# Loading the second product's weights on GpSimd's queue: one hybrid encoder, one core

## The chip, the cores and the metric

The kernel runs on one core of one Trainium2 chip. The metric is the device time of one execution in microseconds (us), from its first to its last instruction and what the launch lays around them.

## The reference

Four post-norm residual layers over x (512 tokens of 1024 features, float32): a bidirectional gated DeltaNet, an MLP, a bidirectional gated linear attention, an MLP.

```python
# DEPTH 2, layer i: token mixer i mod 2, then the MLP; alpha = 4 ** 0.25
x = layernorm(alpha * x + mixer_i(x))             # gated DeltaNet, then gated linear attention
x = layernorm(alpha * x + square(relu(x @ w1)) @ w2)   # w1: 1024 x 4096, w2: 4096 x 1024
```

The change touches the MLPs and the constants of the linear attention.

## The kernel before, in words

Every product is made in full float32 accuracy out of pieces: an operand is split into a high part (a cast on ACT, L90: `wh`, `w2h`, `ah`) and a low part (a subtraction on DVE, L91: `wl`, `w2l`, `al`), and TensorE does three products for one (L109 to L111).

The stages follow one another: DeltaNet up to about 455 us, the first MLP to about 790, linear attention to about 1057, the second MLP to the end. They overlap at the seams.

An MLP (`mlp`) handles its 4096 hidden features in four groups of eight column blocks ("features", f 0 to 7). For a feature, TensorE multiplies the input (`xth`, `xtl`) with a tile of w1 (`wst`, 512 KB, issued by SP at L45, three buffers) into a PSUM bank (`pj`, two of them), and ACT evicts it as relu and square into `h` (L276 and L277). The first four features of the first group are made in halves, since the input arrives in parts. The eighth feature waits for the bank of the sixth, and so on, so a late eviction on ACT holds TensorE.

The second product, of `h` with w2, is done for the groups 0 to 2 by Winograd's form of Strassen's scheme: seven products instead of eight. A group's rows of w2 are four blocks, (i, j) = (0,0), (0,1), (1,1) and (1,0), here A, B, C and D; each is two tiles `w2r` of 512 KB (q = 0 and 1: A0, A1 and so on; E0 and E1 are block (0,0) of the next group), out of a ring of ten. The block sums that the scheme needs are made in place by accumulating DMAs on GpSimd's queue (`plus`, L303, `w2r<-w2r`): first A += B and B += C, later A += C and D += A. Since each reads what a load has brought, it waits for that load, and the second pair waits for the first. Each `w2r` tile is also split into `w2h` and `w2l` (three buffers).

In the first group of an MLP, then, SP loads `wst` tiles and `w2r` tiles in one in-order queue, GpSimd (POOL) loads the layer norm's parameters (`ln`, L173) and issues the accumulations, and ACT has the splits' casts and the evictions in one order. The order on each engine is that of a scheduler, which takes instructions as the code issues them and as their operands come ready. `order` rows below show it; a name in front of an arrow is the tile written, the ones behind it are read.

In the first MLP, `extra` makes the constants of the linear attention at the same time (`GlaConst`): masks `mu` out of a temporary `tmp` that POOL fills (a memset and two affine selects), of which DVE takes the difference to the one before as 8-bit integers (L483 and L485), and two small loads, `gb` and `gcol`, on POOL's queue.

Of the kernel before, what the change touches and what calls it, by code (L numbers as in the profile page):

```python
# [12 lines left out]
AF = mybir.ActivationFunctionType  # L13
ALU = mybir.AluOpType
# [3 lines left out]
P = 128  # L18
# [232 lines left out]
def mlp(c, w1, w2, g, b, out=None, extra=None):  # L251
# [7 lines left out]
    tc, nc = c.tc, c.nc  # L259
    V, A, T = nc.vector, nc.scalar, nc.tensor  # L260
    G = 4
    GF = FF // G // P
    HF = GF // 2
    HT = S // 2
    with c.banks(pj=2, X=2, Y=2, Z=2), tc.tile_pool(name="mlp", bufs=2) as pool:
# [8 lines left out]

        def act(ps, h):
            A.activation(h, ps, AF.Relu)  # L276
            A.activation(h, h, AF.Square)  # L277

        def raw():
            return pool.tile([P, 2, 512], F32, name="w2r", tag="w2r", bufs=10)  # L280

        def load(gi, i, j):
            for q in range(2):
                blocks[i, j, q] = t = raw()
                r = (gi * GF + i * HF + 2 * q) * P
                c.dma(t, w2[r:r + 2 * P, 512 * j:512 * j + 512].rearrange("(k p) n -> p k n", p=P))

        def split(i):

            i_, j_ = {1: (0, 0), 2: (1, 0), 3: (1, 1), 4: (1, 0), 5: (0, 0), 6: (0, 0), 7: (0, 1)}[i]  # L290
            parts[i] = [c.split(blocks[i_, j_, q], [P, 2, 512], pool=ring("w2")) for q in range(2)]

            if i == 1:
                plus((0, 0), (0, 1))
                plus((0, 1), (1, 1))
            elif i == 5:
                plus((0, 0), (1, 1))
                plus((1, 0), (0, 0))
# [6 lines left out]
        def new_h():  # L305
            return [pool.tile([P, HF, S], F32, name="h", tag="h", bufs=3) for _ in range(2)]

        def feature(gi, f, h):
            act(c.proj_cm(w1, (gi * GF + f) * P, "pj"), h[f // HF][:, f % HF, :])

        def pair(src, where="ah"):
            return c.split(src, [P, HF, HT], pool=ring(where))
# [9 lines left out]
        def quarters(h):  # L322
            return [h[j][:, :, HT * i:HT * i + HT] for i in range(2) for j in range(2)]

        def second(gi, h, a, nxt):
# [19 lines left out]
            def fetch(i, j):  # L345
                if gi + 2 < G:
                    load(gi + 1, i, j)

            X, Y = banks("X"), banks("Y")
            load(gi, 1, 0)  # L350
            product(X, a, 1, True)
            for j in range(2):
# [71 lines left out]
        h = new_h()  # L424
        specs = [(c.wcols(w1, f * P, pool=ring("ah") if f == 3 else None), "pj", ("pj", "pj", "X", "X")[f]) for f in range(4)]
        for f, ps in enumerate(c.proj_halves(specs)):
            act(ps, h[0][:, f, :])
        for f in range(4, GF):
            feature(0, f, h)
            if f == 5:  # L430
                load(0, 0, 0)
                load(0, 0, 1)
            if f == 6:
                load(0, 1, 1)
                split(1)
                a = pair(quarters(h)[0])
        if extra:
            extra(lambda: pool.tile([P, P], F32, name="tmp", tag="tmp", bufs=2))
        for gi in range(G - 1):
            more = gi + 2 < G  # L440
            nh = new_h()
            todo = iter(range(GF))

            def nxt():
                f = next(todo)
                feature(gi + 1, f, nh)
                if f == 6 and more:
                    split(1)
                    nxt.a = pair(quarters(nh)[0])

            second(gi, h, a, nxt)
            h, a = nh, nxt.a if more else None
# [13 lines left out]
def sel_masks(c, pool, tmp):  # L466

    nc = c.nc
    out = {}
    prev = None  # L470
    for w in (1, 2, 4, 8, 16, 32, 64, 128):
        f = tmp().rearrange("p (a b) -> p a b", b=w)
        nc.gpsimd.memset(f, 1.0)
        if w < P:
            nc.gpsimd.affine_select(out=f, in_=f, compare_op=ALU.is_ge, fill=0.0, base=0,
                                    pattern=[[-w, P // w], [0, w]], channel_multiplier=1)
            nc.gpsimd.affine_select(out=f, in_=f, compare_op=ALU.is_ge, fill=0.0, base=w - 1,
                                    pattern=[[w, P // w], [0, w]], channel_multiplier=-1)
        fl = f.rearrange("p a b -> p (a b)")
        if w != 2:  # L480
            m = pool.tile([P, P], mybir.dt.uint8, name=f"mu{w}", tag=f"mu{w}", bufs=1)
            if w == 1:
                nc.vector.tensor_copy(m, fl)  # L483
            else:
                nc.vector.tensor_tensor(m, fl, prev, ALU.subtract)  # L485
            out[w // 2] = m
        prev = fl
    return out
# [5 lines left out]
class GlaConst:  # L494


    def __init__(self, c, pool, gate_b, norm_g, tmp):
        nc = c.nc
        self.masks = sel_masks(c, pool, tmp)
        self.gb = pool.tile([P, 2, B_H], F32, name="gb", bufs=1)  # L500
        nc.gpsimd.dma_start(self.gb, gate_b.rearrange("n (h p) -> p n h", p=P), allow_slow_non_contiguous=True)
        self.ngb = pool.tile([P, 2, B_H], F32, name="ngb", bufs=1)
        nc.gpsimd.tensor_scalar(self.ngb, self.gb, -1.0, None, ALU.mult)
        self.gcol = pool.tile([P, B_DV // P], F32, name="gcol", bufs=1)
        nc.gpsimd.dma_start(self.gcol, norm_g.rearrange("(i p) -> p i", p=P), allow_slow_non_contiguous=True)
# [876 lines left out]
def body(tc, nc, a, out):  # L1382
    with contextlib.ExitStack() as es:
        def pool(name, bufs, **kw):
            return es.enter_context(tc.tile_pool(name=name, bufs=bufs, **kw))

        c = Ctx(tc, nc, (pool("const", 1), pool("big", 1), pool("wst", 3), pool("whl", 3), pool("small", 4)))
        x = a["x"][0]
        gdn(c, a["a_w_in"][0], a["a_conv"][0], a["a_alog"][0], a["a_dt_bias"][0], a["a_norm_g"][0],
            a["a_w_out"][0], a["ln1_g"][0], a["ln1_b"][0], x)  # L1390
        with tc.tile_pool(name="gcst", bufs=1) as gp:
            gc = []
            mlp(c, a["mlp_w1"][0], a["mlp_w2"][0], a["ln2_g"][0], a["ln2_b"][0],
                extra=lambda tmp: gc.append(GlaConst(c, gp, a["b_gate_b"][0], a["b_norm_g"][0], tmp)))
            gla(c, gc[0], a["b_w_in"][0], a["b_gate_w2"][0], a["b_w_out"][0], a["ln1_g"][1], a["ln1_b"][1])
        mlp(c, a["mlp_w1"][1], a["mlp_w2"][1], a["ln2_g"][1], a["ln2_b"][1], out=out[0])
# [18 lines left out]
```

## Time and profile before

| | us |
|---|---|
| median of 3 runs | 1401.55 (1400.87 to 1402.34) |
| the profiled execution | 1402.67 |
| its span, first to last instruction | 1401.0 |
| TensorE busy | 1363.1 (97%) |
| VectorE (DVE) busy | 929.5 (66%) |
| ScalarE (ACT) busy | 689.9 (49%) |
| GpSimd (POOL) busy | 122.2 (9%) |

The span is that of one execution taken by the profiler; PE, DVE, ACT, POOL and SP are the five engines. Rows of a timeline give the start, the duration, the engine, the line, the operation and its tiles (out<-in), and in brackets the idle time before it on its engine, with what ended it. Rows of the table of stretches give for each engine the busy time and the count of instructions in a stretch (PE, weight loads of PE, DVE, ACT, POOL), then TensorE's granted clock, the share of time in which the core's 16 DMA engines were busy (a little over 1 is possible), and GB/s. In the DMA part q0 is the queue that GpSimd's DMAs use, q1 the one of SP's; each row has packets, MB and the share of the engines' time. The chain that ended last is followed back from the last instruction.

### The profile page before, as it was taken

To read this page: it belongs to the slowest core of one execution; us is meant where nothing else is said; L and a number is where in the kernel's file an instruction comes from. 1 tells how busy PE (TensorE), PEld (TensorE's weight loads), DVE (VectorE), ACT (ScalarE), POOL (GpSimd) and SP (SyncE) were. 2 spreads that over 40 slices of the span, in tenths; PEclk is the share of its full clock that TensorE was granted. 3 is DMA by queue.
4 is the path that set the end of the run, shared out by engine and by line. 5 is a ranking of instruction groups with operands and counts; after the bars stand their busy time and mean duration, and the time that the engine had idled before them with its cause. 6 is when DMAs were issued, how large, how long until landed. Compare 5 with 4: busy or idle time off the path is not lost.

```text
span 1401.0 us, 20210 instructions
## 1 busy us (share of the span) xinstructions
PE 1363.1 (97%) x7917; PEld 1117.2 (80%) x7917; DVE 929.5 (66%) x1539; ACT 689.9 (49%) x1320; POOL 122.2 (9%) x169
## 2 busy tenths in 40 slices
PE   7999999999999999999999999999999999999997
PEld 6777777777777888888887888888869788888886
DVE  5787787778667365655555577977773555656655
ACT  3776657665633454444443254554433544445430
POOL 5000000000003300100000100000011000001000
PEclk9999999999999999999999999999999999999999
DMA  6312111211133964655422232221218566646121
GB/s 171 76 48 60 47 46 46 61 46 46 47 108 93 295 153 149 143 157 120 105 91 56 82 91 76 61 64 58 91 46 249 152 185 150 165 121 134 48 80 55
DMA packets 154198, 142.62 MB, mean 102 GB/s; under 512 B 9503, under 2 KB 124311, under 8 KB 154103
## 3 DMA queue, kind: packets, MB, share of 16 engines
q1 hardware_dynamic: 145280, 111.89, 26.7%
q0 software_dynamic: 8256, 29.37, 10.8%
q8 instruction: 62, 1.02, 0.3%
q14 instruction: 33, 0.27, 0.1%
q10 hardware_dynamic: 567, 0.08, 0.0%
HBM read 114.05 MB, written 2.10 MB: 83 GB/s over the span
## 4 chain that ended last, share of the span: by engine, by line
PE 58%; issue 23%; DMA 7%; ACT 6%; DVE 3%; POOL 3%; SPq 0%; POOLq 0%; DVEq 0%; ACTq 0%
DMA w2r<-w2r 4%; PE pj L109 4%; PE pj L110 4%; PE pj L111 4%; PE pjv L109 3%; PE pjv L111 3%; PE pjv L110 3%; PE scp L689 2%; PE op L1346 2%; PE pjq L110 1%; DMA wst<-in_mlp_w 1%; PE pjq L111 1%; PE pjq L109 1%; PE op L777 1%; PE lv L1221 1%
## 5 line engine op out<-in xcount | busy, mean ns | idle before, releaser
L91 DVE TENSOR_TENSOR wl<-wst,wh 128x1024 fp32r<-128x1024 f32 x137 | 168.7, 1232 | 197.7 <-ACT wh L90 196.9
L90 ACT CAST wh<-wst 128x1024 fp32r<-128x1024 f32 x137 | 144.0, 1051 | 283.3 <-PE pj L110 174.5
L109 PE MATMUL pj<-xth,wh 128*128 128x512 f32 (+1 forms) x544 | 202.7, 373 | 3.9 <-ACT h L276 3.2
L111 PE MATMUL pj<-xth,wl 128*128 128x512 f32 (+1 forms) x544 | 202.2, 372 | 0.5 <-DVE wl L91 0.5
L110 PE MATMUL pj<-xtl,wh 128*128 128x512 f32 (+1 forms) x544 | 202.1, 372 | 0.4 <-DVE xtl L150 0.4
L91 DVE TENSOR_TENSOR w2l<-w2r,w2h 128x1024 fp32r<-128x1024 f32 x84 | 102.6, 1221 | 69.3 <-ACT w2h L90 69.3
L109 PEld LDWEIGHTS pj<-xth,wh 128*128 128x128 f32 x544 | 102.6, 189 | 22.8 <-ACT h L276 4.5
L111 PEld LDWEIGHTS pj<-xth,wl 128*128 128x128 f32 x544 | 102.6, 189 | 19.0 <-DVE wl L91 1.0
L110 PEld LDWEIGHTS pj<-xtl,wh 128*128 128x128 f32 x544 | 102.9, 189 | 18.6 <-DVE xtl L150 0.8
L90 ACT CAST w2h<-w2r 128x1024 fp32r<-128x1024 f32 x84 | 88.2, 1050 | 58.2 <-DMA w2r<-in_mlp_w 25.6
L303 POOL DMA_DIRECT2D w2r<-w2r x48 | 41.5, 902 | 402.9 <-DVE w2l L91 235.7
L90 ACT CAST ah<-h 128x1024 fp32r<-128x1024 f32 x40 | 42.2, 1054 | 41.1 <-PE pX L110 16.8
L110 PE MATMUL pX<-w2l,ah 128*128 128x512 f32 x144 | 56.1, 390 | 0.0
L109 PE MATMUL pX<-w2h,ah 128*128 128x512 f32 x144 | 56.1, 390 | 0.0
L111 PE MATMUL pX<-w2h,al 128*128 128x512 f32 x144 | 56.1, 390 | 0.0
L109 PE MATMUL pjv<-wh,xth 128*128 128x512 f32 x128 | 54.7, 428 | 0.0
L91 DVE TENSOR_TENSOR al<-h,ah 128x1024 fp32r<-128x1024 f32 x40 | 48.9, 1222 | 5.7 <-ACT ah L90 4.2
L160 ACT ACTIVATE rsy<-rsv 128x1 f32<-128x1 f32 (+1 forms) x28 | 5.6, 201 | 90.9 <-DVE rsv L159 90.9
L111 PE MATMUL pjv<-wh,xtl 128*128 128x512 f32 x128 | 50.2, 392 | 0.0
L110 PE MATMUL pjv<-wl,xth 128*128 128x512 f32 x128 | 49.9, 390 | 0.0
L1169 POOL TENSOR_TENSOR atl<-on,ath 128x512 f16<-128x512 f32 x16 | 20.9, 1308 | 323.2 <-ACT ath L1168 171.5
L109 PE MATMUL pjk<-xth,wh 128*128 128x512 f32 (+1 forms) x112 | 42.0, 375 | 0.5 <-ACT wh L90 0.5
(434 smaller groups left out, 3440.5 us busy)
## 6 DMA issues: line engine op xcount, KB each, us to landing
wst<-in_mlp_w SPq DMA_DIRECT2D x80, 512.0 KB, 4.1
w2r<-in_mlp_w SPq DMA_DIRECT2D x48, 512.0 KB, 4.4
w2r<-w2r POOLq DMA_DIRECT2D x48, 512.0 KB, 5.7
wst<-in_a_w_in SPq DMA_DIRECT2D x32, 512.0 KB, 4.0
wst<-in_b_w_in SPq DMA_DIRECT2D x32, 256.0 KB, 3.1
wst<-in_a_w_out SPq DMA_DIRECT2D x8, 512.0 KB, 3.8
wst<-in_b_w_in SPq DMA_DIRECT2D x8, 512.0 KB, 3.8
wst<-in_b_w_out SPq DMA_DIRECT2D x8, 512.0 KB, 3.6
```

The source lines that it names most:

```text
L90: nc.scalar.copy(hi, src)
L91: nc.vector.tensor_tensor(lo, src, hi.bitcast(F32), ALU.subtract)
L109: mm(ps, ah, bh, start=start, stop=False, **kw)
L110: mm(ps, ah, bl, start=False, stop=False, **kw)
L111: mm(ps, al, bh, start=False, stop=stop, **kw)
L160: nc.scalar.activation(y, v, AF.Ln)
L303: nc.gpsimd.dma_start(blocks[a + (q,)], blocks[b + (q,)], accum_op=ALU.add)
L689: T.matmul(ps[:, n, :], kh[:, sl], qh[:, sl], start=True, stop=True)
L777: T.matmul(ops, l, r, start=i == 0, stop=i == len(mm) - 1)
L1169: G.tensor_tensor(atl[:, us, :], at, ath[:, us, :], ALU.subtract)
L1221: T.matmul(ps[:, u, :, :], lhs[:, u, :], cols(rhs, u, s, i), start=True, stop=True)
L1346: T.matmul(op[:, n, :], l, r, start=i == 0, stop=i == len(mm) - 1)
```

## The change

The loads of `w2r` go from SP to GpSimd (`nc.gpsimd.dma_start` in `load_part`). The first group's loads are no longer issued at the sixth and seventh feature: A and B are issued after the first four evictions, C after the next two, each in a context `issue_after` with the eviction's last instruction. The mask differences are made by GpSimd alone, in place in float32, and cast to 8 bits by it too.

```diff
         def act(ps, h):
             A.activation(h, ps, AF.Relu)
-            A.activation(h, h, AF.Square)
+            return A.activation(h, h, AF.Square)
...
         def load(gi, i, j):
             for q in range(2):
+                load_part(gi, i, j, q)
+
+        def load_part(gi, i, j, q, after=None):
+            with c.tc.issue_after(after.ins) if after else contextlib.nullcontext():
                 blocks[i, j, q] = t = raw()
                 r = (gi * GF + i * HF + 2 * q) * P
-                c.dma(t, w2[r:r + 2 * P, 512 * j:512 * j + 512].rearrange("(k p) n -> p k n", p=P))
+                nc.gpsimd.dma_start(t, w2[r:r + 2 * P, 512 * j:512 * j + 512].rearrange("(k p) n -> p k n", p=P))
...
         def feature(gi, f, h):
-            act(c.proj_cm(w1, (gi * GF + f) * P, "pj"), h[f // HF][:, f % HF, :])
+            return act(c.proj_cm(w1, (gi * GF + f) * P, "pj"), h[f // HF][:, f % HF, :])
...
         for f, ps in enumerate(c.proj_halves(specs)):
-            act(ps, h[0][:, f, :])
+            load_part(0, 0, f // 2, f % 2, after=act(ps, h[0][:, f, :]))
         for f in range(4, GF):
-            feature(0, f, h)
-            if f == 5:
-                load(0, 0, 0)
-                load(0, 0, 1)
+            done = feature(0, f, h)
+            if f in (4, 5):
+                load_part(0, 1, 1, f % 2, after=done)
             if f == 6:
-                load(0, 1, 1)
                 split(1)
                 a = pair(quarters(h)[0])
...
             if w == 1:
-                nc.vector.tensor_copy(m, fl)
+                nc.gpsimd.tensor_copy(m, fl)
             else:
-                nc.vector.tensor_tensor(m, fl, prev, ALU.subtract)
+                nc.gpsimd.tensor_tensor(prev, fl, prev, ALU.subtract)
+                nc.gpsimd.tensor_copy(m, prev)
```

On POOL, the head of the first MLP before: the four `ln` loads are followed by masks, the two small loads and, between masks, the four accumulations (`w2r<-w2r`).

```order
L503 TENSOR_SCALAR ngb<-gb 128x8
L303 DMA w2r<-w2r 128x1024
L473 MEMSET tmp 128x128
L303 DMA w2r<-w2r 128x1024
L475 AFFINE_SELECT tmp<-tmp 128x128
L477 AFFINE_SELECT tmp<-tmp 128x128
L303 DMA w2r<-w2r 128x1024
L473 MEMSET tmp 128x128
L303 DMA w2r<-w2r 128x1024
L475 AFFINE_SELECT tmp<-tmp 128x128
```

After, on POOL at the same place: w2r_6133 and w2r_6137 are B0 and B1, w2r_6172 and w2r_6207 are C0 and C1, w2r_6353 is D0. The six loads before these rows, A0 to C1, stand directly behind the `ln` loads.

```order
L307 DMA w2r_6133<-w2r_6172 128x1024
L307 DMA w2r_6137<-w2r_6207 128x1024
L479 AFFINE_SELECT tmp_6291<-tmp_6291 128x128
L477 AFFINE_SELECT tmp_6297<-tmp_6297 128x128
L485 CAST mu1_6295<-tmp_6291 128x128
L479 AFFINE_SELECT tmp_6297<-tmp_6297 128x128
L475 MEMSET tmp_6301 128x128
L504 DMA gb_6341<-in_b_gate_b 128x8x1
L477 AFFINE_SELECT tmp_6301<-tmp_6301 128x128
L508 DMA gcol_6345<-in_b_norm_g 128x2x1
L479 AFFINE_SELECT tmp_6301<-tmp_6301 128x128
L290 DMA w2r_6353<-in_mlp_w2 128x2x512
```

D0's load, on SP's queue before, now stands behind the fourth accumulation and the first masks; D1 and the next group's E0 and E1 follow between later masks.

On POOL, the head of the second MLP after; the rows before it are the four `ln` loads. w2r_10986 to w2r_11068 are A0, A1, B0, B1, C0 and C1, w2r_11158 and w2r_11160 are D0 and D1.

```order
L290 DMA w2r_10986<-in_mlp_w2 128x2x512
L290 DMA w2r_10990<-in_mlp_w2 128x2x512
L290 DMA w2r_10994<-in_mlp_w2 128x2x512
L290 DMA w2r_10998<-in_mlp_w2 128x2x512
L290 DMA w2r_11033<-in_mlp_w2 128x2x512
L290 DMA w2r_11068<-in_mlp_w2 128x2x512
L307 DMA w2r_10986<-w2r_10994 128x1024
L307 DMA w2r_10990<-w2r_10998 128x1024
L290 DMA w2r_11158<-in_mlp_w2 128x2x512
L307 DMA w2r_10994<-w2r_11033 128x1024
L307 DMA w2r_10998<-w2r_11068 128x1024
L290 DMA w2r_11160<-in_mlp_w2 128x2x512
```

Before, only `ln` loads and accumulations stood there; D0 now comes between the first pair of accumulations and the second.

On ACT, the head of the first MLP, from the second feature's square on, before:

```order
L277 ACTIVATE h<-h 128x512
L90 CAST w2h<-w2r 128x1024
L276 ACTIVATE h<-pj 128x512
L90 CAST wh<-wst 128x1024
L277 ACTIVATE h<-h 128x512
```

and after, from the fifth feature's eviction on:

```order
L276 ACTIVATE h<-pj 128x512
L277 ACTIVATE h<-h 128x512
L90 CAST w2h<-w2r 128x1024
L90 CAST wh<-wst 128x1024
L276 ACTIVATE h<-pj 128x512
L277 ACTIVATE h<-h 128x512
```

The single cast of `w2h` in both is D0's. It moved from in front of the third feature's eviction to behind the fifth feature's square, in front of a `wst` cast and the sixth feature's eviction. The order on TensorE is the same in both kernels.

## The prediction

> **What bounds the kernel now.** I read the page first, for the share of each engine and the landing times of the DMAs; then the table of stretches, to find where TensorE is not full; then the timelines of PE, ACT and POOL in those stretches, and the chain that ended last.
>
> ```profile
> PE 1363.1 (97%) x7917; PEld 1117.2 (80%) x7917; DVE 929.5 (66%) x1539; ACT 689.9 (49%) x1320; POOL 122.2 (9%) x169
> L1169 POOL TENSOR_TENSOR atl<-on,ath 128x512 f16<-128x512 f32 x16 | 20.9, 1308 | 323.2 <-ACT ath L1168 171.5
> w2r<-in_mlp_w SPq DMA_DIRECT2D x48, 512.0 KB, 4.4
> w2r<-w2r POOLq DMA_DIRECT2D x48, 512.0 KB, 5.7
> ...
> 455.00:485.00 30.00, 29.02 (x172) 24.91 (x170) 12.06 (x17) 13.94 (x19) 12.17 (x24) 1.00 1.08 304
> 530.00:570.00 40.00, 40.00 (x178) 32.92 (x176) 21.75 (x23) 18.10 (x22) 3.42 (x4) 1.00 0.55 147
> 1060.00:1100.00 40.00, 37.25 (x224) 33.35 (x225) 12.77 (x12) 18.06 (x24) 3.45 (x4) 0.96 0.98 279
> ```
>
> TensorE is busy 97% of the span, and in the steady part of an MLP (530 to 570) all of 40 us: nothing that this change touches can be gained there. In the two heads of the MLPs, where the first group's features are made, TensorE loses 1 and 2.75 us, and the DMA engines are full (shares 1.08 and 0.98, against 0.55). So the change is worth what it does in those two heads. The losses, on PE:
>
> ```profile
> 478.39 0.50 PE L109 MATMUL pj<-xth,wh 128*128 128x512 f32 x1 [0.24 <-ACT h L276]
> 479.66 0.50 PE L111 MATMUL pj<-xth,wl 128*128 128x512 f32 x1 [0.53 <-DVE wl L91]
> 485.31 0.50 PE L109 MATMUL pj<-xth,wh 128*128 128x512 f32 x1 [0.36 <-ACT h L276]
> ...
> 1087.98 0.39 PE L111 MATMUL pj<-xth,wl 128*128 128x512 f32 x1
> 1090.96 0.80 PE L109 MATMUL pj<-xth,wh 128*128 128x512 f32 x1 [2.59 <-ACT h L276]
> ...
> 1094.03 0.39 PE L110 MATMUL pj<-xtl,wh 128*128 128x512 f32 x1
> 1094.25 0.39 PE L111 MATMUL pj<-xth,wl 128*128 128x512 f32 x1
> ```
>
> A matmul lasts 0.39 us but the next starts after 0.22 to 0.23 (1094.03 to 1094.25), so an idle counted from its end hides 0.16 more, and the first matmul behind it is 0.11 longer. Each of the three small idles costs its length and 0.27: 0.51 + 0.80 + 0.63 = 1.9 us in the first head. In the second, 1087.98 to 1090.96 is 2.98 in place of 0.23, and the seven starts up to 1094.03 take 3.07 in place of 1.59, since behind that long idle the granted clock is lower (0.96 in the mean of the stretch): 2.75 + 1.48 = 4.2 us. Together 6.1 us could be won, 0.44% of the time.
>
> What stands behind them, on ACT, and in the chain:
>
> ```profile
> 471.66 1.05 ACT L90 CAST w2h<-w2r 128x1024 fp32r<-128x1024 f32 x1 [7.96 <-DMA w2r<-in_mlp_w]
> 483.71 1.05 ACT L90 CAST wh<-wst 128x1024 fp32r<-128x1024 f32 x1 [4.71 <-DMA wst<-in_mlp_w]
> ...
> 1081.25 1.05 ACT L90 CAST w2h<-w2r 128x1024 fp32r<-128x1024 f32 x1 [8.08 <-DMA w2r<-in_mlp_w]
> 1089.37 1.04 ACT L90 CAST wh<-wst 128x1024 fp32r<-128x1024 f32 x1 [2.21 <-DMA wst<-in_mlp_w]
> 1090.32 0.59 ACT L276 ACTIVATE h<-pj 128x512 f32<-128x512 f32 x1
> ...
> 1071.20 18.07 DMA wst<-in_mlp_w
> ```
>
> The bank that TensorE needs is freed by the eviction at 1090.32, which stands on ACT behind a cast of a first-product tile (`wst`) that took 18.07 us to land, behind second-product tiles in SP's queue. ACT had also stood 8 us for D0, the third second-product block's first half.
>
> **The change part by part.** First the loads. All 48 `w2r` loads leave SP and are issued by POOL. In the order, the words that are to tie them to evictions leave no wait on them: they stand right behind the four `ln` loads. What remains of the tie is only their place in POOL's order, costed at nothing. Behind them POOL has the accumulating DMAs, and, in the first head, masks, two small loads and only then D0.
>
> ```profile
> 449.48 1.09 POOL L173 DMA_DIRECT2D ln<-in_ln_g  x2 [0.30 <-POOL xt L194]
> 450.56 1.06 POOL L173 DMA_DIRECT2D ln<-in_ln_b  x2
> 455.46 0.94 POOL L501 DMA_DIRECT2D gb<-in_b_gate_b  x1
> 456.54 0.71 POOL L505 DMA_DIRECT2D gcol<-in_b_norm_g  x1
> 463.21 0.96 POOL L303 DMA_DIRECT2D w2r<-w2r  x1 [0.28 <-issue]
> 471.48 0.86 POOL L303 DMA_DIRECT2D w2r<-w2r  x1 [5.37 <-DMA w2r<-w2r]
> 474.53 0.85 POOL L303 DMA_DIRECT2D w2r<-w2r  x1 [1.97 <-DMA w2r<-w2r]
> 475.08 0.65 POOL L475 TENSOR_SCALAR_AFFINE_SELECT tmp<-tmp 128x128 f32<-128x128 f32 x1
> 475.80 0.34 POOL L477 TENSOR_SCALAR_AFFINE_SELECT tmp<-tmp 128x128 f32<-128x128 f32 x1
> 476.52 0.20 POOL L473 MEMSET tmp<- 128x128 f32 x1 [0.39 <-DVE mu L485]
> ...
> 476.17 0.29 DVE L485 TENSOR_TENSOR mu<-tmp 128x128 uint8<-128x128 f32 x1 [8.60 <-POOL tmp L477]
> ```
>
> The head of the second MLP has the accumulations without masks between them:
>
> ```profile
> 1057.46 1.09 POOL L173 DMA_DIRECT2D ln<-in_ln_g  x2 [0.30 <-POOL xt L194]
> 1068.18 0.89 POOL L303 DMA_DIRECT2D w2r<-w2r  x1 [8.58 <-DMA w2r<-in_mlp_w]
> 1071.25 0.87 POOL L303 DMA_DIRECT2D w2r<-w2r  x1 [2.18 <-DVE wl L91]
> 1076.79 0.85 POOL L303 DMA_DIRECT2D w2r<-w2r  x1 [4.67 <-DMA w2r<-w2r]
> ```
>
> First head, D0. The `ln` issues end at 451.6. Six loads at 0.53 (an `ln` load) to 0.86 (an accumulation) are issued by 455 to 457. The first accumulation waits for B0's landing: in the second head that was 10.7 us behind the first `ln` issue (1057.46 to 1068.18), with the same bytes in the engines, so here it goes out at 460.2. Its landing took 8.3 us (463.21 to 471.48) and 8.6 (1068.18 to 1076.79), and releases the third, at about 468.6; the fourth came 3.05 behind the third, so 471.7, and is issued by 472.6. Behind it, before D0, POOL now has five affine selects (two at 0.65 or somewhat more, three at 0.34: 2.6), a memset (0.20), the loads gb and gcol (0.94 + 0.71) and a cast to the mask, which POOL doesn't have in the trace: between DVE's 0.29 and the 1.31 of a 128x512 tile on POOL, a quarter of which is 0.33; I take 0.45, nearer the quarter. That is 4.9, so D0 is issued at 477.5. It lands after 4.4 (a load's median) to 5.7 us (this queue's own median for 512 KB): 481.9 to 483.2, and I take 483.1, since the queue is the one that it goes through. If the fourth accumulation goes out two microseconds earlier, it is 480 to 481.
>
> When is D0 due? D0's cast now stands on ACT in front of the cast of the next group's first tile and the eviction of the sixth feature, which frees the bank of the eighth. Without its three idles the first head would start the eighth at 485.31 - 1.9 + 0.11 = 483.5. From the cast at 483.71 to the matmul at 485.31 are 1.60 us; D0's own cast adds 0.96. So D0 is due at 480.9. At 483.1 TensorE idles 2.2 us. The clock's share lies between 0.11 (behind 0.53 of idle) and 1.48 (behind 2.59); I take 0.9, nearer the latter. Loss 2.2 + 0.3 + 0.9 = 3.4, where it was 1.9: **+1.5 us**, with ends of -1.9 (D0 in time) and +4 (D0 at 485).
>
> The masks. Six tensor_tensors and one cast leave DVE, 7 x 0.29 = 2.0 us at least, all in a stretch where DVE is busy 12 of 30 us; their worth is the wait of 8.60 that they put in front of DVE's splits, of which TensorE saw 0.80. It is gone, and is in the 1.9 above. POOL gets six tensor_tensors and seven casts, at 0.33 to 1.31 each, behind D0 but for one: 4 to 17 us more, with nobody waiting but the next layer and the first group's later accumulations. POOL is busy 12 of 30 us in that stretch, which is cover enough; if it is not, the loads behind them pay what they run over.
>
> Second head. D0 stands on POOL behind the two first accumulations: issued at about 1072.1, lands behind the second one. The third goes out at 1076.8 on the landing of the first, and the second lands about 3 us later, near 1079.8; D0's own 0.52 MB at the first head's 304 GB/s are 1.7 us more: 1081.5. Due: on ACT a cast, an eviction, a square (about as long) and another cast (1.05 + 0.59 + 0.59 + 1.05 = 3.3) stand between it and the `wst` cast, which must start 1.6 before 1088.2: 1083.3. In time by nearly 2 us. The `wst` tile itself is due at 1086.6. SP, with no `w2r` loads in its queue, has nothing in front of it; but it is issued at the same 1071.20 (its buffer is freed then), and shares the engines with POOL's queue:
>
> ```profile
> q0 software_dynamic: 200, 0.75, 94.2%
> q1 hardware_dynamic: 200, 0.12, 13.4%
> ...
> q0 software_dynamic: 320, 1.05, 52.4%
> q1 hardware_dynamic: 647, 1.23, 48.0%
> ...
> q1 hardware_dynamic: 615, 0.31, 105.5%
> ```
>
> The first two rows are the stretch 468 to 472: both queues put through 200 packets, POOL's of 4 KB, SP's of 512 B. They take turns packet by packet, and the `wst` tile's 1024 packets go at 50 in a us, where alone (third stretch, 1094 to 1095) they go at 615. The second pair is 1060 to 1067, where POOL's `ln` loads of 2 KB rows went as packets of 4 KB, so I give its `w2r` loads 128 packets each. Four accumulations (512 packets, 10.2 us at 50) and D0 (128, 1.7 us) let through 640 of the 1024; 128 more go beside D1 (1.7), 256 alone in 0.4. Before's first accumulation landed at 1076.79 and needs 2.6 for its 128 packets, so they begin near 1074: 1074 + 10.2 + 1.7 + 1.7 + 0.4 = 1088.0. Gaps in POOL's queue before the third accumulation, at 615 packets in a us, would bring it back to 1086 or 1087. I take 1088.0: an idle of 1.4, and with 0.3 and a clock's share of 0.4 a loss of 2.1, where it was 4.2: **-2.1 us**, with ends of -4.2 and +0.7.
>
> The Trainium skill ("DMA: Bandwidth & Descriptors", section "Issuing engines are not separate DMA queues") says that DMAs of all issuers end on the same 16 engines, and that several issuers save only the issuing time; by that alone the second head keeps its 4.2 and the sum is +1.5, still inside the forecast's own range. Its section "Queues, rings and completion order" has each engine go round its queues packet by packet, with which the trace's 200 and 200 agree.
>
> Steady part: POOL's order has the loads and the accumulations in the order in which before's buffers came free; TensorE is at 40.00 of 40 there. Costed at nothing; what hides it is that the loads are issued a group ahead.
>
> Sum: +1.5 - 2.1 = -0.6 on the profiled run's 1402.67, which lies 1.1 above the median of 1401.55. Median after: 1401.0.
>
> **The rivals.** *Both heads come clean.* D0 is issued two us earlier in the first (accumulations alone in the queue, without SP's 2 KB loads beside them, landing in 5.7 rather than 8.3), so it is due in time, and `wst` lands by 1086.6. For it: 5.7 is the median; against: the bytes in the head are the same, and the engines are full. -1.9 and -4.2 at most, -4.6 with a small idle in each: 1397.0. Chance 0.22.
>
> *Slower: the small packets starve.* The same exchange packet by packet decides it, in the other way: POOL's queue, never empty from 1060 to 1090, lets `wst` through later than SP's own order did. If it lands after 1089.3 (fewer than 384 of its packets going beside D1 or in gaps), the second head loses as much as before or 0.7 more; in the first head the tile for the next group lands late by the same and D0 at 484.4, an idle of about 3.5 with 1.8 for restart and clock, 5.3 in place of 1.9. +0.7 + 3.4 = +4.1: 1405.6. For it: 0.98 and 1.08 of DMA share, and 200 against 200; against: the waits of the accumulations leave gaps in POOL's queue. Chance 0.28.
>
> *POOL's queue in the steady part.* A load behind an accumulation waits up to 8 us with it, and one of them comes late at each group's start: 1 to 5 us in all, 1404. Against: TensorE has never waited for them there. Chance 0.04.
>
> *The tie acts after all.* The change says that loads follow evictions; if they did, the first would go out behind the first eviction, near 460 and not at 451.6, D0 8 us later, and both heads lose: some +10, 1411. The order shows no wait. Chance 0.02.
>
> **How the numbers follow.** About 0.2%, 2.8 us, is what a measurement of this kernel tells from no change. The forecast (1398.8 to 1404.3) has 0.44, and counts as the same. Faster: 0.22. Slower: 0.28 + 0.04 + 0.02 = 0.34. The range takes in most of the first rival and about half of the second: 1396.8 to 1405.6.
>
> **What would show it.** In the profile after: no `w2r` load on SP; D0's cast on ACT at about 483 in the first head, with the idle before it ended by that load, and TensorE idle some 2 us just behind; `wst` of the second head cast at 1088 (its time shifted by what the first head lost) and not 18 us behind its issue; DVE no longer waiting for POOL. I am wrong if D0 is cast before 481, if `wst` still takes 18 us, or if TensorE has new idles after the heads.

## The result, and the profile after

The changed kernel is slower: 1408.08 us in the median of six runs (1405.19 to 1409.98), against 1401.23 of six runs of the kernel before on the same chip. The ratio is 1.0042, 95% interval 1.0029 to 1.0055, some 6 us. It lies above the predicted range of 1396.8 to 1405.6. The profiled execution took 1407.43, its span is 1405.7.

The table of stretches of the changed kernel, and behind it the same first row (14 to 18 us) of the kernel before:

```profile
14.00:18.00 4.00, 3.26 (x16) 2.48 (x17) 3.69 (x6) 2.16 (x4) 1.88 (x3) 0.69 0.48 109
455.00:485.00 30.00, 30.00 (x192) 27.30 (x191) 9.28 (x8) 13.14 (x18) 14.85 (x22) 1.00 1.00 282
485.00:495.00 10.00, 4.24 (x12) 3.06 (x11) 3.99 (x3) 5.18 (x7) 8.18 (x15) 0.75 0.77 235
530.00:570.00 40.00, 40.00 (x178) 32.91 (x176) 22.61 (x24) 18.95 (x22) 6.87 (x9) 1.00 0.52 152
1060.00:1100.00 40.00, 39.01 (x264) 35.56 (x263) 16.85 (x22) 18.84 (x27) 14.16 (x19) 1.00 0.88 244
```

```profile
14.00:18.00 4.00, 3.39 (x28) 2.99 (x29) 3.55 (x6) 2.04 (x4) 2.08 (x4) 1.00 0.49 126
```

The three small idles of the first head are gone (TensorE at 30.00 of 30 up to 485), the second head is almost full (39.01 of 40, and what is missing lies at the seam with the attention), and the steady part is full as before. In place of all that stands one hole: in the ten microseconds from 485, TensorE works 4.24, and its clock is granted at 0.75. The first row is an event of its own: this execution had a stretch of slow clock at 15 us that before's did not have. It lies 430 us ahead of anything that the change touches and shifts all later times of this profile by 1.8 us, some 2 us by the first head.

Matched matmul by matmul against before, the changed kernel is 2.1 us late from 457 on (2.5 just ahead of it: a small idle of before's at 457 is gone too), 0.8 us late at 482 (two small idles won), 8.65 us late behind the hole, then constant through the steady part and within 0.1 through the attention, 8.57 late at the start of the second head and 4.75 late from 1100 on. So from 457 on the first head costs 6.5 us net and the second gives 3.8 back, against this one profile of before.

The hole, on PE and ACT of the changed kernel:

```profile
491.46 0.80 PE L109 MATMUL pj<-xth,wh 128*128 128x512 f32 x1 [5.76 <-ACT h L276]
492.06 0.63 PE L110 MATMUL pj<-xtl,wh 128*128 128x512 f32 x1
...
462.07 1.05 ACT L90 CAST w2h<-w2r 128x1024 fp32r<-128x1024 f32 x1 [6.08 <-DMA w2r<-in_mlp_w]
488.92 1.04 ACT L90 CAST w2h<-w2r 128x1024 fp32r<-128x1024 f32 x1 [12.07 <-DMA w2r<-in_mlp_w]
...
1092.29 1.05 ACT L90 CAST w2h<-w2r 128x1024 fp32r<-128x1024 f32 x1 [6.74 <-DMA w2r<-in_mlp_w]
1095.50 1.04 ACT L90 CAST wh<-wst 128x1024 fp32r<-128x1024 f32 x1
```

D0's cast comes at 488.92, after ACT had stood 12.07 us for its load; the eviction behind it frees the bank for the matmul at 491.46. In the second head the first-product tile's cast at 1095.50 has no wait in brackets at all. And the way of D0, on POOL:

```profile
452.00 1.09 POOL L173 DMA_DIRECT2D ln<-in_ln_g  x2 [0.30 <-POOL xt L194]
453.08 1.07 POOL L173 DMA_DIRECT2D ln<-in_ln_b  x2
454.14 4.28 POOL L290 DMA_DIRECT2D w2r<-in_mlp_w  x6
467.23 0.94 POOL L307 DMA_DIRECT2D w2r<-w2r  x1 [8.81 <-DVE wl L91]
...
475.06 0.86 POOL L307 DMA_DIRECT2D w2r<-w2r  x1 [3.31 <-DMA w2r<-w2r]
478.59 0.86 POOL L307 DMA_DIRECT2D w2r<-w2r  x1 [2.67 <-DMA w2r<-w2r]
...
484.85 0.82 POOL L290 DMA_DIRECT2D w2r<-in_mlp_w  x1
```

The six first loads go out at once, then POOL stands 8.8 us before the first accumulation, 3.3 before the third, 2.7 before the fourth, and has 6.3 us of masks and small loads up to D0.

### The profile page after: what moved, and what is told of

The parts are those of the page before. It is cut to its first block, busy times and chain, and to the rows that moved or that the text cites. A ratio compares the mean times of both kernels' runs of the same rounds, so it can differ in the third digit from the quotient of the medians.

```text
span 1405.7 us, 20187 instructions
## 1 busy us (share of the span) xinstructions
PE 1366.4 (97%) x7917; PEld 1120.6 (80%) x7917; DVE 928.6 (66%) x1532; ACT 690.3 (49%) x1320; POOL 165.1 (12%) x230
## 4 chain that ended last, share of the span: by engine, by line
PE 70%; issue 13%; ACT 7%; DMA 5%; DVE 3%; POOL 2%; SPq 0%; DVEq 0%; POOLq 0%; ACTq 0%
PE pj L109 6%; PE pj L111 6%; PE pj L110 6%; PE pjv L109 3%; PE pjv L111 3%; PE pjv L110 3%; DMA w2r<-in_mlp_w 2%; PE pX L110 2%; PE pX L111 2%; PE pX L109 2%; PE scp L692 2%; PE op L1349 2%; DMA w2r<-w2r 1%; PE pjq L110 1%; PE pZ L110 1%
## 5 line engine op out<-in xcount | busy, mean ns | idle before, releaser
L290 POOL DMA_DIRECT2D w2r<-in_mlp_w x48 | 35.5, 742 | 115.2 <-DVE w2l L91 79.7
```

The source lines that it names most:

```text
L290: nc.gpsimd.dma_start(t, w2[r:r + 2 * P, 512 * j:512 * j + 512].rearrange("(k p) n -> p k n", p=P))
```

## The experiments

The theory: the whole loss is that of D0, which POOL issues too late in the first MLP, and the gain is in the two heads, by the masks in the first and by the free hardware queue in the second. The rivals: GpSimd's mask work is what costs; the software queue costs as such, wherever it is used; the late tile is another one. Each kernel was timed in turn with the kernel before on the same chip, except where a single run is named. The spread of the kernel before over these sessions was 1398.2 to 1406.3, so a ratio's interval is about a tenth of a per cent to each side.

**Second MLP alone on GpSimd's queue** (from the kernel before):

```diff
-                c.dma(t, w2[...])
+                (nc.sync if extra else nc.gpsimd).dma_start(t, w2[...])
```

> Before, with the second-product loads on GpSimd's queue in the second MLP alone; the first MLP's loads and the masks as before. Theory (the loss is D0's late load in the first head, the gain is the second head's, where the first-product tile no longer stands behind second-product loads): the first head as before, the second head's idle of 2.6 us and its slow clock gone, 3.9 us faster than before, 1397.3, ratio 0.997. Rival (loads by GpSimd's software queue cost time wherever they are): not faster than before, 1401 to 1404.

Measured: 1400.89 against 1402.64, ratio 0.9989 (0.9979 to 0.9999). Faster, if only just clear of 1, so GpSimd's queue does not cost wherever it is used, but by less than half of what was expected. In its profile the second head does come clean, 3.8 us better than in the profile of before; why the times show less is taken up at the second profile of before, below.

**Masks alone** (from the kernel before): the three changed lines of `sel_masks`, nothing else.

> Before, with the masks made by GpSimd alone; all loads on SP. Theory: DVE no longer waits for GpSimd, of which TensorE sees 0.8 us at most: 0 to 1 us faster, 1400.4 to 1401.2, nothing new idle. Rival (the masks' longer work on GpSimd is what costs, through the accumulations behind it): 2 to 6 us slower, 1403 to 1407, with the accumulations late.

Measured: 1399.46, ratio 0.9980 (0.9968 to 0.9993). GpSimd's mask work by itself costs nothing; that rival falls. (What it costs in front of D0 is another question, which this kernel does not ask: its loads are on SP.) The gain is larger than I gave it. Matched against before, its matmuls gain 2.4 us in the first head, where I had counted only the 0.8 that stood directly behind DVE's wait: the other two small idles went with it, and a fourth one at 457.11, 0.15 long and worth 0.4, that the prediction passed over.

**D0 and D1 of the first MLP on SP** (from the changed kernel):

```diff
-                nc.gpsimd.dma_start(t, w2[...])
+                (nc.sync if extra and gi == 0 and (i, j) == (1, 0) else nc.gpsimd).dma_start(t, w2[...])
```

> The changed kernel with D0 and D1 of the first MLP's first group loaded by SP. Theory: D0 no longer stands behind accumulations and masks, so the first head's idle of 5.8 us goes; what is left is the second head's gain and the masks': 1396 to 1398, 4 us faster than before. Rival (GpSimd's masks or its queue as such): still slower than before, 1403 to 1407.

Measured: 1400.62, ratio 0.9984 (0.9973 to 0.9995), 6 to 8 us better than the changed kernel, but only some 2 us better than before, where 4 were expected. Moving D0 and D1 out of POOL's queue takes the loss in time away. The first head is not clean, though, in the profiled execution, which took 1402.36 (the twelve lie between 1396.46 and that): matched against before, it still loses 3 us there. PE and ACT:

```profile
486.78 0.50 PE L109 MATMUL pj<-xth,wh 128*128 128x512 f32 x1 [2.99 <-ACT h L276]
488.22 0.63 PE L110 MATMUL pj<-xtl,wh 128*128 128x512 f32 x1
...
485.18 1.04 ACT L90 CAST wh<-wst 128x1024 fp32r<-128x1024 f32 x1 [6.66 <-DMA wst<-in_mlp_w]
```

Now it is a first-product tile that comes late, at 485.18, sharing SP's queue with D0 and D1 and the engines with GpSimd's packets; which of the two held it, this run does not show.

**Masks and small loads behind the first group** (from the changed kernel):

```diff
-        if extra:
-            extra(lambda: pool.tile([P, P], F32, name="tmp", tag="tmp", bufs=2))
         for gi in range(G - 1):
+            if extra and gi == 1:
+                extra(lambda: pool.tile([P, P], F32, name="tmp", tag="tmp", bufs=2))
```

The order then has D0 between the second and the third accumulation.

> The changed kernel with the masks and the two small loads made behind the first group instead of ahead of it, so that D0 stands on GpSimd directly behind the first two accumulations, as in the second MLP. Theory with the masks as the main delay: D0 is issued 5 us or more earlier, the first head's idle falls from 5.8 to under 1 us: 1397 to 1399. Theory with the accumulations' waits as the main delay: an idle of 3 us or more stays, 1400 to 1403.

Measured: 1398.83, ratio 0.9985 (0.9974 to 0.9996). PE, ACT and POOL in its first head:

```profile
479.95 0.50 PE L109 MATMUL pj<-xth,wh 128*128 128x512 f32 x1 [1.74 <-ACT h L276]
...
477.41 1.05 ACT L90 CAST w2h<-w2r 128x1024 fp32r<-128x1024 f32 x1 [5.20 <-DMA w2r<-in_mlp_w]
...
467.62 1.05 POOL L290 DMA_DIRECT2D w2r<-in_mlp_w  x1
```

D0 goes out at 467.62, where the changed kernel has it at 484.85, and TensorE idles 1.74 in place of 5.76. The idle lies between the two theories, the time in the range of the first. The kernel skipped two things at once, the masks and the wait for the third and fourth accumulation, so this run does not part them. D0's cast also stands one feature further ahead on ACT here, in front of the fifth feature's eviction, so it is due earlier than in the changed kernel.

**No tie** (from the changed kernel): the plain calls at the sixth and seventh feature, on GpSimd's queue.

```diff
-            load_part(0, 0, f // 2, f % 2, after=act(ps, h[0][:, f, :]))
+            act(ps, h[0][:, f, :])
...
-            done = feature(0, f, h)
-            if f in (4, 5):
-                load_part(0, 1, 1, f % 2, after=done)
+            feature(0, f, h)
+            if f == 5:
+                load(0, 0, 0)
+                load(0, 0, 1)
             if f == 6:
+                load(0, 1, 1)
```

> The changed kernel with the tie undone: no context around the loads, which the code issues at the sixth and seventh feature as before does. The order and the waits on all five engines come out the same as in the changed kernel, so the theory (the tie does nothing) expects the changed kernel's time, 5 to 7 us slower than before, with an idle of about 6 us in the first head. Rival (the tie delays something that the order does not show): clearly faster than that.

Measured: 1406.40, ratio 1.0033 (1.0021 to 1.0045): the changed kernel's time within the intervals. The tie does nothing, as the order says. As its program is the changed kernel's, this is a second profile of it, without the slow clock at the start. PE, ACT and POOL:

```profile
489.49 0.79 PE L109 MATMUL pj<-xth,wh 128*128 128x512 f32 x1 [5.82 <-ACT h L276]
...
460.08 1.05 ACT L90 CAST w2h<-w2r 128x1024 fp32r<-128x1024 f32 x1 [6.13 <-DMA w2r<-in_mlp_w]
486.94 1.04 ACT L90 CAST w2h<-w2r 128x1024 fp32r<-128x1024 f32 x1 [12.14 <-DMA w2r<-in_mlp_w]
...
463.56 0.94 POOL L307 DMA_DIRECT2D w2r<-w2r  x1 [7.20 <-DMA w2r<-in_mlp_w]
470.39 0.86 POOL L307 DMA_DIRECT2D w2r<-w2r  x1 [2.64 <-DMA w2r<-w2r]
474.60 0.86 POOL L307 DMA_DIRECT2D w2r<-w2r  x1 [3.34 <-DMA w2r<-w2r]
480.84 0.82 POOL L290 DMA_DIRECT2D w2r<-in_mlp_w  x1
```

The same hole, 2 us earlier: its matmuls are 1.3 us ahead of before's at 482 and 6.4 behind once the hole is past, so 7.6 us lost in the hole.

Its second head, on ACT and PE:

```profile
1090.46 1.05 ACT L90 CAST w2h<-w2r 128x1024 fp32r<-128x1024 f32 x1 [6.30 <-DMA w2r<-in_mlp_w]
1095.25 0.50 PE L109 MATMUL pj<-xth,wh 128*128 128x512 f32 x1 [0.62 <-ACT h L276]
```

ACT waits there for D0 and then works without a pause up to the eviction that ends the idle of 0.62: what is left is D0's load, not a first-product tile.

**First MLP alone on GpSimd's queue** (from the changed kernel):

```diff
-                nc.gpsimd.dma_start(t, w2[...])
+                (nc.gpsimd if extra else nc.sync).dma_start(t, w2[...])
```

> The changed kernel with the second MLP's loads back on SP: the loads on GpSimd's queue and the masks in the first MLP alone. Theory (D0 behind accumulations, masks and small loads costs 6.5 us in the first head, the second head's gain is gone): 6 to 8 us slower than before, 1407 to 1410. Rival (the loss is spread over both MLPs): 2 to 4 us slower.

Measured: 1407.61, ratio 1.0037 (1.0025 to 1.0050), 5 us slower than before, between the two expectations. All of the loss is in the first MLP, the only one that differs from before; the ratio is 0.0004 above that of the kernel without the tie, less than the intervals, so the second head's gain does not show here. Its profiled execution has a span of 7699.5 us and shows nothing of this, so the kernel was run once more for its profile:

> The changed kernel with the second MLP's loads back on SP, once more for its profile. Theory: the first head as in the changed kernel (D0 cast at about 487, an idle of about 6 us, 6 to 7 us lost with what follows it), the second head as in before, losing 2.6 to 4.2 us.

That single run took 1408.86. PE in its first head, ACT in its second:

```profile
490.20 0.80 PE L109 MATMUL pj<-xth,wh 128*128 128x512 f32 x1 [6.61 <-ACT h L276]
...
1095.21 1.04 ACT L90 CAST wh<-wst 128x1024 fp32r<-128x1024 f32 x1 [1.45 <-DMA wst<-in_mlp_w]
```

The hole is there (6.61). In the second head, which has before's program, its matmuls lose as much as before's: the shift against before goes only from 6.2 to 6.1.

**The kernel before, once more**, a single run for its profile:

> The kernel before once more, for a second profile. If the second head's loss of 4.2 us is the same in each execution, its idle is again 2.4 us or more with the clock low behind it; if it differs from run to run, the idle is shorter or without the slow clock, as in the kernel with the masks alone, and the second head's gain is worth 1 to 3 us in the mean rather than 3.9.

It took 1399.08, with a span of 1397.4, 3.6 us shorter than the first profile of the same kernel, and all of that lies in the second head. The stretch, ACT, POOL, and the DMA queues from 1080 to 1082 in this profile:

```profile
1060.00:1100.00 40.00, 39.73 (x242) 35.24 (x241) 13.11 (x12) 18.35 (x25) 3.45 (x4) 1.00 1.00 284
...
1086.89 1.05 ACT L90 CAST wh<-wst 128x1024 fp32r<-128x1024 f32 x1
...
1070.04 0.89 POOL L303 DMA_DIRECT2D w2r<-w2r  x1 [10.20 <-DMA w2r<-in_mlp_w]
1078.51 0.85 POOL L303 DMA_DIRECT2D w2r<-w2r  x1 [6.28 <-DMA w2r<-w2r]
...
q1 hardware_dynamic: 900, 0.50, 82.0%
q0 software_dynamic: 37, 0.09, 21.9%
```

The tile that took 18.07 us in the first profile is cast here at 1086.89 without a wait. What differs in the two traces is a race of 2 us. The accumulations go out 1.9 us later (1070.04 against 1068.18, 1078.51 against 1076.79), and between the first pair's end and the second pair's start SP's queue has the engines nearly to itself: 900 packets against 37 in two microseconds, most of them the tile's 1024 of 512 B. In both profiles the tile's packets begin only at about 1080, behind loads in 2 KB packets in SP's queue. Where the second pair's packets begin with less than half of the tile through, as in the first profile, the rest goes between them:

```profile
q0 software_dynamic: 285, 1.04, 74.8%
q1 hardware_dynamic: 784, 0.70, 31.9%
```

That is the first profile of before from 1081 to 1088: 7 us for 784 packets, of which 564 are of 512 B and 202 of 2 KB. They do not go one for one throughout, as GpSimd's queue has gaps; from 1081 to 1083 it was 95 against 156. That the accumulations' start decides it is read from these two traces; no run moved it alone. So the second head's 4.2 us is lost in some executions of the kernel before and not in others. With masks alone, whose second MLP is before's, it lost 2.35 us of idle and no clock:

```profile
1088.65 0.50 PE L109 MATMUL pj<-xth,wh 128*128 128x512 f32 x1 [2.35 <-ACT h L276]
```

**D0 and D1 with the first six loads** (from the changed kernel):

```diff
             if f == 6:
+                load(0, 1, 0)
                 split(1)
...
-            load(gi, 1, 0)
+            if gi:
+                load(gi, 1, 0)
```

> The changed kernel with the first group's D0 and D1 issued with the first six loads, ahead of the accumulations, in both MLPs; everything else as changed. Theory: D0 lands near 468 in the first head, long before it is due; both heads nearly clean, 4 to 6 us faster than before, ratio 0.996. Rival (what is late in the first head is the software queue's landing as such, or the tiles behind): an idle of 2 us or more stays in the first head, ratio 0.999 or above.

Measured: 1400.39, ratio 0.9993 (0.9982 to 1.0004): the loss is gone, but nothing won, where 4 to 6 us were expected. PE and ACT:

```profile
479.14 0.50 PE L109 MATMUL pj<-xth,wh 128*128 128x512 f32 x1 [1.13 <-ACT h L276]
1094.59 0.50 PE L109 MATMUL pj<-xth,wh 128*128 128x512 f32 x1 [1.54 <-ACT h L276]
...
477.55 1.05 ACT L90 CAST wh<-wst 128x1024 fp32r<-128x1024 f32 x1 [4.23 <-DMA wst<-in_mlp_w]
1092.99 1.04 ACT L90 CAST wh<-wst 128x1024 fp32r<-128x1024 f32 x1 [5.36 <-DMA wst<-in_mlp_w]
```

D0 no longer holds TensorE; the first-product tiles do, in both heads. Here and in the kernel with D0 on SP, a tile that came earlier left another one late.

**The `ln` loads on SP** (from the changed kernel), so that A0 stands first in GpSimd's queue:

```diff
-        par = c.load_ln(g, b, lambda i: pool.tile([P, 512], F32, name=f"ln{i}", bufs=1))
+        par = c.load_ln(g, b, lambda i: pool.tile([P, 512], F32, name=f"ln{i}", bufs=1), nc.sync)
...
-            self.nc.gpsimd.dma_start(t, src[...])
+            (eng or self.nc.gpsimd).dma_start(t, src[...])
```

> The changed kernel with the MLPs' ln loads on SP, so that A0 stands first in GpSimd's queue. Theory (the first accumulation went out late because A0 and B0 land behind the ln loads in one software queue, and D0 behind it): the first accumulation 4 us earlier, D0 as well, the first head's idle 1 to 3 us instead of 5.8: 1402 to 1405. Rival (the software queue's own start and landing are what is late): the first accumulation still 13 us or more behind the first load's issue, an idle of 5 us or more, 1406 to 1409.

Measured: 1407.60, ratio 1.0039 (1.0025 to 1.0053), no better than the changed kernel. POOL, ACT and PE:

```profile
449.31 4.37 POOL L290 DMA_DIRECT2D w2r<-in_mlp_w  x6 [0.30 <-POOL xt L194]
459.36 0.96 POOL L307 DMA_DIRECT2D w2r<-w2r  x1 [5.68 <-DVE w2l L91]
...
478.72 0.72 POOL L290 DMA_DIRECT2D w2r<-in_mlp_w  x1
...
483.00 1.04 ACT L90 CAST w2h<-w2r 128x1024 fp32r<-128x1024 f32 x1 [7.17 <-DMA w2r<-in_mlp_w]
...
485.54 0.80 PE L109 MATMUL pj<-xth,wh 128*128 128x512 f32 x1 [6.46 <-ACT h L276]
```

The first accumulation goes out 4.2 us earlier than without the tie (459.36 against 463.56), as the theory says, and D0's cast comes 3.9 earlier (483.00 against 486.94). The idle stays all the same, 6.46: in this kernel's order D0's cast stands one feature further ahead on ACT, in front of the fifth feature's eviction and no longer behind its square, so it is also due a feature earlier. The idle and the time fall into the rival's ranges, though not for its reason, a late first accumulation. The expectation of the time was wrong, since I had not asked where the scheduler would then put D0's cast; of the accumulations it was right.

**The two good parts together** (from the kernel before): the masks by GpSimd alone, and the second MLP's loads on GpSimd's queue; the first MLP's loads stay on SP.

> Before with the two parts that the theory holds for good: the masks by GpSimd alone, and the second MLP's second-product loads on GpSimd's queue; the first MLP's loads stay on SP. Theory: the first head clean as with the masks alone (2.4 us), the second clean as with the second MLP's loads alone (up to 3.9 us): 4 to 6 us faster than before, ratio 0.996. Rival (the two gains are one and the same run-to-run spread): ratio 0.998 to 0.999, as each alone.

Measured: 1397.32, ratio 0.9966 (0.9953 to 0.9978), 4.6 us faster than before and 9 to 11 us faster than the changed kernel. Its stretches:

```profile
455.00:485.00 30.00, 30.00 (x181) 26.87 (x181) 11.50 (x10) 14.88 (x20) 19.50 (x37) 1.00 1.09 301
1060.00:1100.00 40.00, 39.11 (x232) 34.62 (x231) 13.19 (x11) 20.02 (x27) 7.86 (x11) 1.00 0.98 277
```

TensorE has no hole in the first head and one idle of 0.89 us in the second, again behind D0's cast.

This kernel and the one without the tie differ in one thing alone, the queue of the first MLP's `w2r` loads, and were timed in the same session: 1397.32 with SP's, 1406.40 with GpSimd's. Of these 9.1 us, the matched matmuls of the two profiles put 8.3 into the first head.

## Why the prediction was wrong

- **What bounds the kernel** was right: nothing moved in the steady part (40.00 of 40 in both), all of it in the two heads.
- **The tie costed at nothing** was right, and shown: without it the order is the same, and the time too.
- **First head, D0.** The mechanism was right: D0 behind accumulations, masks and small loads, its cast in front of the sixth feature's eviction, TensorE idle behind it. The size was not, and this is the step that failed: the term for D0, forecast at +1.5 us, came out at 6.3 to 6.5. In the second profile of the changed kernel, without the slow clock at the start, D0 was cast at 486.9 in place of 483.1. The first accumulation went out at 463.6, not 460.2: I had carried over the second head's 10.7 us behind the first `ln` issue, since the bytes are the same, but in before the loads ran beside the `ln` tiles, on SP's queue; behind them, in one queue, A0 is cast at 460.1 in place of 453.4. The kernel with the `ln` loads on SP confirms this term: 459.4, with A0 cast at 455.1. The third accumulation came 6.8 later (8.4 forecast), the fourth 4.2 (3.05), D0's issue 6.2 (5.8), its landing 6.1 (5.6). That adds up to a cast 3.8 us later than forecast. When it was due was right (2.55 us from the cast to the matmul behind it, 2.56 forecast), so TensorE idled 5.8 us for 2.2, and the slow clock behind it cost 2.2 in this profile and 2.5 in the first, not 0.9. The prediction's upper end of +4 for this term was too low as well: it assumed D0 at 485.
- **Second head.** It came out nearly clean, better than the residual loss of 2.1 forecast, and not for the forecast's reason: the `wst` tile, forecast late by 1.4, was in time, and D0, forecast in time by nearly 2, left the idle of 0.62 in the kernel without the tie. And "where it was 4.2" was wrong as a statement about the kernel: I read a race's losing side out of one execution. Four profiles have before's program in the second head; matched, it lost 4.2, 4.1 (first MLP alone on GpSimd's queue), 2.6 (masks alone) and 0.4 us (before once more). By the times, moving these loads is worth 1 to 2 us: 0.11% alone, 0.14% on top of the masks, each uncertain by a tenth of a per cent or more.
- **The masks** were right in kind. The sum had already counted the three small idles, 1.9 us, as won, but gave the masks only 0.8 of it; alone they won 2.4, the fourth idle at 457.11 included.
- **The rivals.** The packet-by-packet rival (small packets starve) fits the second head of before and the late `wst` tiles of the kernels with D0 early or on SP, though no run tested it there. It did not decide the changed kernel, where no cast in either head waits more than 0.15 us for `wst`. That kernel was slower for the forecast's own reason, sized too small.
- **Which queue the loads go through.** The Trainium skill ("DMA: Bandwidth & Descriptors", section "Issuing engines are not separate DMA queues") says that starting DMAs from several engines saves only the time that it takes to start them. The runs here do not agree with that as the whole of it: the same bytes took 1397.32 or 1406.40 us by the queue of the first MLP's loads alone, through what stands in front of what in each queue.

What stays open: how the loss of D0 parts between the waits for the accumulations and the masks. The trace of the changed kernel puts 10 us between the second and the fourth accumulation and 6.3 between the fourth and D0, but no run moved one without the other. How often the second head's race is lost is not known beyond the four profiles.

## What to carry to other kernels

A load that moves to another queue arrives by what stands before it there, and by the waits of each instruction in that queue: count them for the load that is due first, and don't take over a landing from a queue in which it ran beside the others. Where DMA engines are full, look for the tile that will be late next before moving one forward; and look where the scheduler puts its consumer. Before a stall of one profile is booked as a gain, see a second execution of the same kernel.

## What the hardware showed that was not expected

- The same program came out in the second head 3.8 us apart in two executions (3.6 in the whole span), with a difference of 2 us in the start of its accumulating DMAs.
- The slow clock behind an idle is not fixed in length: behind 2.35 us of idle (masks alone) no matmul ran at the slow pitch, behind 2.59 six did (1.5 us lost), behind 5.76 twelve (2.5 us lost), but behind 6.61 (first MLP alone on GpSimd's queue) six again. Nor does it always begin with the first matmul: behind 2.99 us, in the kernel with D0 on SP, the first took 0.50 and not 0.80, and the seven from 487.37 to 490 took 0.63 in place of 0.39.
- GpSimd's loads of 512 KB with 2 KB rows go as packets of 4 KB, as estimated from the `ln` loads. The changed kernel from 461 to 466, where 469 of the 524 packets are of 4 KB and the others of 4 bytes:

```profile
q0 software_dynamic: 524, 1.92, 100.2%
```
